# Two MLP down-projections computed with seven half-size matrix products instead of eight in most of their steps

## The chip, the cores and the metric

The kernel runs on one core of a Trainium2 chip. The metric is the device time of one execution in microseconds (us), of which several are timed and the median is given. TensorE multiplies matrices and accumulates in eight PSUM banks of 128 x 512 float32 values; VectorE (DVE in the profile) and ScalarE (ACT) do elementwise work; SyncE's queue (SP) starts the transfers from device memory. Each engine takes its instructions strictly from its own queue, and engines wait for each other through semaphores.

## The reference, cut to what matters

Two layers of a hybrid block act on x of 256 tokens by 1024 channels. Each layer mixes tokens (an mLSTM and two attentions) and then runs an MLP:

```python
mix = jnp.concatenate([hm, ha, hl], axis=-1)
x = x + mix @ w_out                                     # 1024 -> 1024
h2 = rms_norm(x, g_mlp_norm)
x = x + jnp.square(jax.nn.relu(h2 @ w_up)) @ w_down     # 1024 -> 4096 -> 1024
```

All of it is float32. The change is in the last product, `@ w_down`, alone.

## The kernel before, in words

**Three products for one.** TensorE is fed with a rounded float32 format. Each operand is therefore split in a high part (a rounded copy) and a low part (what the rounding left), and `mm3` (L192 to L195) issues three matmuls for one product: high x high (L193), low x high (L194) and high x low (L195). Every weight is split on the chip: `stream` has ScalarE write the high part `wh` (L182) and VectorE the low part `wl` (L183), 128 x 1024 values at a time, in the order in which the products take the pieces, up to six pieces ahead. The split pieces live in a ring of seven slots (`hlp`), which a piece leaves when its last matmul is through. The raw weights come from device memory in jobs of 1 MB (two pieces each) into three buffers `raw` (L165), on SyncE's queue.

**The MLP** is a loop of 18 rounds, j = 0 to 17. In rounds 0 to 15 a step of w_up makes 256 of the 4096 hidden channels: two blocks of 128 channels by 256 tokens, each a sum over 8 blocks of input channels, so 2 x 8 x 3 = 48 matmuls with 256 columns into one PSUM bank `up`. Then the hidden values are made: L931 (ACT) `rr` = relu(up), L932 (DVE) `hf` = max(up, 0) x rr, L933 (ACT) `hrh` = the rounded square, L934 (DVE) `hrl` = hf - hrh. In rounds 2 to 17 a step of w_down uses the hidden values made two rounds before (LAG = 2): two blocks b of 128 hidden channels, two halves m of the tokens, two halves n of the 1024 output channels, 2 x 2 x 2 x 3 = 24 matmuls with 512 columns. They accumulate over all 16 steps in four banks `acc`, one for each (m, n). So TensorE does step 0, 1, 2 of w_up, then w_down 0, w_up 3, w_down 1, and so on to w_down 14 and 15.

After the last step `update` (L947) scales each bank by r2, which holds the norm's factor per token, and adds it to the running x (`xs`). In the first layer TensorE goes on with transposes of xs (`xtp`, L327) and with `latp`, the first product of the next layer; `xh` and `xl` are the split halves of the transposed x. In the second layer the halves go to device memory.

**PSUM.** Four of the eight banks belong to the group "big" (here `acc`), four to "sm" (here `up` and `xtp`).

**Order of the work.** The program is written in the order above; a scheduler then sets the order in each engine's queue and places the waits, by what each instruction reads and writes and by when pool slots come free. The rows of that order are shown where a step of the prediction rests on them.

Of the kernel before, what the change touches and what calls it, by code (L numbers as in the profile page):

```python
# [10 lines left out]
F32 = mybir.dt.float32  # L11
F32R = mybir.dt.float32r
# [107 lines left out]
def hybrid_kernel(ctx: ExitStack, tc: tile.TileContext, x: bass.AP, xt: bass.AP, pos: bass.AP,  # L120
# [10 lines left out]
    def sb(shape, name, dt=F32, bufs=1, tag=None):  # L131
        return tp.tile([128] + list(shape), dt, name=name, tag=tag or name, bufs=bufs)
# [36 lines left out]

    def stream(i):  # L170
        while state["split"] < min(i + SPLIT_AHEAD + 1, len(pieces)):
            _, _, j, c, n = pieces[state["split"]]
# [3 lines left out]
            r = raw[j][:, c:c + n]  # L176
            if j == 0:
                hl[state["split"]] = (r,)
            else:
                h = hlp.tile([128, PW], F32R, name="wh", tag="wh")  # L180
                lo = hlp.tile([128, PW], F32R, name="wl", tag="wl")
                A.activation(h[:, :n], r, AF.Copy)  # L182
                V.tensor_sub(lo[:, :n], r, h[:, :n].bitcast(F32))  # L183
# [8 lines left out]
    def mm3(o, lh, ll, rh, rl, start, stop):  # L192
        T.matmul(o, lh, rh, start=start, stop=False)  # L193
        T.matmul(o, ll, rh, start=False, stop=False)  # L194
        T.matmul(o, lh, rl, start=False, stop=stop)  # L195
# [264 lines left out]
    for l in range(L):  # L460
# [444 lines left out]
        xh, xl, half = made_["x"]  # L905


        r2 = sb([2], "r2")
        acc = []
        hs = {}  # L910
        hrh = sb([4, 2, S], "hrh", F32R, tag="xh2")
        hrl = sb([4, 2, S], "hrl", F32R, tag="xl2")
        rr = sb([1024], "rr", tag="dB").rearrange("p (c b t) -> p c b t", c=2, b=2)
        hf_ = sb([2, 2, S], "hf", tag="yc")
        for j in range(16 + LAG):
            if j < 16:
                up = sm([2, S], "up")
                if j == 0:
# [5 lines left out]
                    acc = [big("acc") for _ in range(2)]  # L924
# [5 lines left out]
                r, hf, hh, hlo = rr[:, j % 2], hf_[:, j % 2], hrh[:, j % 4], hrl[:, j % 4]  # L930
                A.activation(r, up, AF.Relu)  # L931
                V.scalar_tensor_tensor(hf, up, 0.0, r, op0=OP.max, op1=OP.mult)  # L932
                A.activation(hh, r, AF.Square)  # L933
                V.tensor_sub(hlo, hf, hh.bitcast(F32))  # L934
                hs[j] = (hh, hlo)
            if j >= LAG:
                i = j - LAG
                ws = [weights(l, "dn", 2 * i + b) for b in range(2)]

                def bank(n, m):  # L940
                    down(acc[m][n], *hs[i], (0, 1), ws, m, n, i == 0, i == 15)

                def update(n, m):
                    w = 256 if l == L - 1 and (n, m) == NM[-1] else 512
                    for c0 in range(0, 512, w):
                        c = slice(n * 512 + c0, n * 512 + c0 + w)
                        V.scalar_tensor_tensor(xs[:, m, c], acc[m][n][:, c0:c0 + w], r2[:, m:m + 1], xs[:, m, c],  # L947
                                               op0=OP.mult, op1=OP.add)
                        if l == L - 1:
                            nc.sync.dma_start(out[:, m, c], xs[:, m, c])  # L950

                if i < 15:
                    for n, m in NM:
                        bank(n, m)
                else:
                    made = last_rows(bank, update, None if l == L - 1 else pr[l + 1][:, P_MIX:P_MIX + 8])

# [70 lines left out]
```

## Time and profile before

| what | value |
|---|---|
| median of 3 runs | 624.45 us (624.13 to 624.69) |
| the profiled execution's own time | 624.25 us |
| its span, from first to last instruction | 622.5 us |
| granted TensorE clock | 1.00 |
| TensorE busy (PE) | 611.1 us, 98% |
| weight loads into TensorE (PEld) | 542.9 us, 87% |
| VectorE busy (DVE) | 398.6 us, 64% |
| ScalarE busy (ACT) | 334.8 us, 54% |
| weight splits on VectorE (L183) | 196 instructions, 233.4 us |

A row of a timeline gives the start in us from the start of the span, the duration, the engine, line, operation, tiles and shapes, how many instructions are merged in the row, and in brackets how long the engine had idled before and what ended that. Matmuls and elementwise instructions overlap their neighbours on the same engine: the next one starts before the recorded end of the one before. In this text the time from one start to the next, of instructions that wait for nothing, is called the **pitch**.

### The profile page before, as it was taken

How to read it: one execution, taken by the hardware profiler on the slowest of the kernel's cores; microseconds unless marked ns; L12 is line 12 of the kernel's file. 1: busy time of each engine (PE TensorE's matmuls, PEld its weight loads, DVE VectorE, ACT ScalarE, POOL GpSimd, SP SyncE). 2: the span in 40 equal slices, each digit the busy share in tenths (PEclk: the TensorE clock that was granted, in tenths of full speed). 3: DMA queues.
4: the chain of work that ended last, by engine and by line, in shares of the span. 5: the costliest groups of instructions: out<-in, count | busy, mean ns of one | idle time of the engine just before them, and what ended most of it. 6: DMA issues, size and time to landing. Idle time of an engine off the chain costs nothing.

```text
span 622.5 us, 9831 instructions
## 1 busy us (share of the span) xinstructions
PE 611.1 (98%) x3850; PEld 542.9 (87%) x3850; DVE 398.6 (64%) x759; ACT 334.8 (54%) x565; POOL 39.6 (6%) x91
## 2 busy tenths in 40 slices
PE   6999999999999999999999999999999999999997
PEld 5988878889998989989899897888998998988985
DVE  4889876767555555555587996786765555555542
ACT  4876885465444444444367777653744444444430
POOL 7852000000000000000000000000000000000000
PEclk9999999999999999999999999999999999999999
DMA  8775221455465564654445642235456465564601
GB/s 294 300 301 197 101 102 69 151 188 203 144 207 192 181 222 139 211 195 169 159 149 215 204 136 73 98 111 185 179 185 218 140 211 195 171 221 151 203 2 67
DMA packets 17327, 106.39 MB, mean 171 GB/s; under 512 B 2304, under 2 KB 2816, under 8 KB 5504
## 3 DMA queue, kind: packets, MB, share of 16 engines
q1 hardware_dynamic: 16992, 105.75, 48.7%
q8 instruction: 30, 0.49, 0.3%
q14 instruction: 17, 0.14, 0.1%
q10 hardware_dynamic: 288, 0.02, 0.0%
HBM read 104.71 MB, written 1.05 MB: 170 GB/s over the span
## 4 chain that ended last, share of the span: by engine, by line
PE 89%; POOL 5%; DVE 3%; issue 1%; ACT 1%; DVEq 0%; POOLq 0%
PE acc L194 12%; PE acc L195 12%; PE acc L193 12%; PE up L193 9%; PE up L194 9%; PE up L195 9%; DVE wl L183 2%; PE vp L194 1%; PE op L193 1%; PE vp L193 1%; PE vp L195 1%; PE op L195 1%; PE op L194 1%; PE lsc L419 1%; PE qkp L194 1%
## 5 line engine op out<-in xcount | busy, mean ns | idle before, releaser
L183 DVE TENSOR_TENSOR wl<-raw,wh 128x1024 fp32r<-128x1024 f32 (+2 forms) x196 | 233.4, 1207 | 142.7 <-ACT wh L182 138.5
L182 ACT ACTIVATE wh<-raw 128x1024 fp32r<-128x1024 f32 (+2 forms) x196 | 200.3, 1043 | 173.9 <-PE acc L194 93.3
L193 PE MATMUL up<-xh,wh 128*128 128x256 f32 x480 | 134.2, 280 | 0.1
L194 PE MATMUL up<-xh,wl 128*128 128x256 f32 x480 | 134.0, 279 | 0.0
L195 PE MATMUL up<-xl,wh 128*128 128x256 f32 x480 | 133.9, 279 | 0.0
L195 PE MATMUL acc<-wl,hrh 128*128 128x512 f32 x256 | 101.3, 396 | 0.0
L193 PE MATMUL acc<-wh,hrh 128*128 128x512 f32 x256 | 101.3, 396 | 0.0
L194 PE MATMUL acc<-wh,hrl 128*128 128x512 f32 x256 | 101.3, 396 | 0.0
L193 PEld LDWEIGHTS up<-xh,wh 128*128 128x128 f32 x480 | 90.3, 188 | 1.7 <-PE xtp L327 0.5
L194 PEld LDWEIGHTS up<-xh,wl 128*128 128x128 f32 x480 | 90.2, 188 | 1.2
L195 PEld LDWEIGHTS up<-xl,wh 128*128 128x128 f32 x480 | 90.3, 188 | 0.0
L195 PEld LDWEIGHTS acc<-wl,hrh 128*128 128x128 f32 x256 | 48.1, 188 | 11.5
L194 PEld LDWEIGHTS acc<-wh,hrl 128*128 128x128 f32 x256 | 48.1, 188 | 10.3
L193 PEld LDWEIGHTS acc<-wh,hrh 128*128 128x128 f32 x256 | 48.1, 188 | 10.4
L931 ACT ACTIVATE rr<-up 128x512 f32<-128x512 f32 x32 | 19.1, 596 | 52.1 <-PE up L195 52.1
L932 DVE SCALAR_TENSOR_TENSOR hf<-up,rr 128x512 f32<-128x512 f32 x32 | 22.1, 691 | 33.2 <-ACT rr L931 33.2
L193 PE MATMUL acc<-wh,mh 128*128 128x512 f32 x64 | 25.9, 404 | 0.0
L195 PE MATMUL acc<-wl,mh 128*128 128x512 f32 x64 | 25.3, 396 | 0.0
L194 PE MATMUL acc<-wh,ml 128*128 128x512 f32 x64 | 25.3, 395 | 0.0
L934 DVE TENSOR_TENSOR hrl<-hf,hrh 128x512 fp32r<-128x512 f32 x32 | 21.9, 685 | 0.1
L933 ACT ACTIVATE hrh<-rr 128x512 fp32r<-128x512 f32 x32 | 19.8, 619 | 0.0
L193 PE MATMUL qkp<-xh,wh 128*128 128x256 f32 x64 | 18.6, 291 | 0.2 <-ACT scr L693 0.2
(351 smaller groups left out, 957.1 us busy)
## 6 DMA issues: line engine op xcount, KB each, us to landing
raw<-in_wts_dram SPq DMA_DIRECT2D x91, 1024.0 KB, 4.8
raw<-in_wts_dram SPq DMA_DIRECT2D x2, 740.0 KB, 5.7
raw<-in_wts_dram SPq DMA_DIRECT2D x2, 576.0 KB, 5.3
xts<-in_xt_dram SPq DMA_DIRECT2D x4, 256.0 KB, 4.4
raw<-in_wts_dram SPq DMA_DIRECT2D x4, 256.0 KB, 4.7
xs<-in_x_dram SPq DMA_DIRECT2D x1, 1024.0 KB, 10.5
raw<-in_wts_dram SPq DMA_DIRECT2D x2, 512.0 KB, 3.5
raw<-in_wts_dram SPq DMA_DIRECT2D x2, 478.0 KB, 7.0
```

The lines of the kernel that those rows point to most:

```text
L182: A.activation(h[:, :n], r, AF.Copy)
L183: V.tensor_sub(lo[:, :n], r, h[:, :n].bitcast(F32))
L193: T.matmul(o, lh, rh, start=start, stop=False)
L194: T.matmul(o, ll, rh, start=False, stop=False)
L195: T.matmul(o, lh, rl, start=False, stop=stop)
L419: T.matmul(sc[j][:, i], qT(2 * i + j, m), kT(2 * i + j, m + 1), start=False, stop=True, skip_group_check=True)
L931: A.activation(r, up, AF.Relu)
L932: V.scalar_tensor_tensor(hf, up, 0.0, r, op0=OP.max, op1=OP.mult)
L933: A.activation(hh, r, AF.Square)
L934: V.tensor_sub(hlo, hf, hh.bitcast(F32))
```

## The change

Write A for the hidden values of a step in four blocks, A(m, b) for token half m and channel block b, and B(b, n) for the weights. Before, each output quarter is C(m, n) = A(m, 0) B(0, n) + A(m, 1) B(1, n): eight products. In steps 0 to 13 of each MLP seven products of sums take their place (the form of Strassen's method with few additions that Winograd gave). With

- U4 = A(1,0) - A(0,0), U5 = A(0,1) - A(0,0), U6 = U4 + A(0,1), U7 = A(1,1) - U6,
- t0 = -B(0,0) - B(0,1), t1 = -B(0,1) - B(1,1), t2 = B(1,1) - t0, t3 = t2 + B(1,0),

the products are P1 = A(1,0) B(0,0), P2 = A(1,1) B(1,0), P6 = U6 t2, P7 = U4 t1, P4 = A(0,1) t3, P5 = U5 t0, P3 = U7 B(1,1), taken in this order, and C(1,0) = P1 + P2, C(0,0) = P4 + P1 - P6 - P7, C(0,1) = P5 - P1 + P6 + P7, C(1,1) = P3 + P5 - P1 + P6.

Each product has a PSUM bank of its own, in which it accumulates over the fourteen steps: P1, P2 and P6 in the group "sm", so that one bank is left there for `up`, the other four in "big". After step 13 the parts that several outputs share are added to xs (`into`); steps 14 and 15 are done with eight products as before, added into the banks P4, P2, P5 and P3, each of which by then holds what is still to be added of one quarter.

The sums of the weights (`dn_part`) and of the hidden values are made by VectorE. They are split in high and low parts afterwards, so that a step of w_down has four pieces: a (512 columns, B(0,0)), b (1024: B(1,1), B(1,0)), d (1024: t2, t3), c (1024: t0, t1). The hidden values are squared into float32 (`us`), seven blocks of 128 columns are formed and split into `hrh` and `hrl`; the step that made `hf` from the PSUM bank is gone. Ring, raw buffers, lookahead in pieces, and the bytes moved are unchanged.

```diff
+SEVEN = 14
+DN_PARTS = {"a": 512, "b": 1024, "d": 1024, "c": 1024, "e": 1024}
+LAST = (((0, 0), 4, ((0, "e", 0), (2, "b", 1))), ((0, 1), 2, ((1, "e", 0), (3, "b", 1))),
+        ((1, 0), 5, ((0, "e", 1), (2, "b", 0))), ((1, 1), 3, ((1, "e", 1), (3, "b", 0))))
+PRODUCTS = ((1, 0, "a", 0), (2, 2, "b", 1), (6, 5, "d", 0), (7, 3, "c", 1), (4, 1, "d", 1), (5, 4, "c", 0),
+            (3, 6, "b", 0))
...
-    return w["w_down"][pc[1] * 128:(pc[1] + 1) * 128]
+    b = w["w_down"][pc[1] * 256:(pc[1] + 1) * 256].reshape(2, 128, 2, 512)
+    return np.concatenate([b[0, :, 0], b[0, :, 1], b[1, :, 1], b[1, :, 0]], axis=1)
...
+                if pc[0] == "dn":
+                    pieces += [(l, (*pc, part), len(jobs), 0, DN_PARTS[part])
+                               for part in ("abdc" if pc[1] < SEVEN else "eb")]
...
+    def dn_part(j, part):
+        r = raw[j]
+        if part in "ae":
+            return r[:, :DN_PARTS[part]]
+        if part == "b":
+            return r[:, 1024:]
+        if part == "d":
+            t = sums[j] = sb([2048], "tsum", tag="mix")
+            V.scalar_tensor_tensor(t[:, :1024], r[:, :1024], -1.0, r[:, 512:1536], op0=OP.mult, op1=OP.subtract)
+            V.tensor_sub(t[:, 1024:1536], r[:, 1024:1536], t[:, :512])
+            V.tensor_add(t[:, 1536:], t[:, 1024:1536], r[:, 1536:])
+            return t[:, 1024:]
+        return sums.pop(j)[:, :1024]
...
+        us = [sb([8, 128], "us", tag=t) for t in ("yc", "qkT")]
...
+        def product(n, i, ai, part, bi, first, last):
+            if n not in prod:
+                prod[n] = ps.tile([128, 512], F32, name=f"P{n}", tag="sm" if n in (1, 2, 6) else "big", bufs=4)
+            wh, wl = weights(l, "dn", i, part)
+            hh, hlo = hs[i]
+            c = slice(bi * 512, bi * 512 + 512)
+            mm3(prod[n], hh[:, ai], hlo[:, ai], wh[:, c], wl[:, c], first, last, skip_group_check=n == 5)
...
-                V.scalar_tensor_tensor(hf, up, 0.0, r, op0=OP.max, op1=OP.mult)
-                A.activation(hh, r, AF.Square)
-                V.tensor_sub(hlo, hf, hh.bitcast(F32))
+                A.activation(u[:, 0:4].rearrange("p (b h) t -> p b (h t)", b=2), r, AF.Square)
+                if j < SEVEN:
+                    V.tensor_sub(u[:, 4:6], u[:, 1:3], u[:, 0:1].to_broadcast([128, 2, 128]))
+                    V.tensor_add(u[:, 6], u[:, 4], u[:, 2])
+                    V.tensor_sub(u[:, 7], u[:, 3], u[:, 6])
+                    src = u[:, 1:]
+                else:
+                    src = u[:, :4]
+                    hh, hlo = hh[:, :4], hlo[:, :4]
+                A.activation(hh, src, AF.Copy)
+                V.tensor_sub(hlo, src, hh.bitcast(F32))
...
+            i = j - LAG
+            if 0 <= i < SEVEN:
+                for p in PRODUCTS:
+                    product(p[0], i, *p[1:], i == 0, i == SEVEN - 1 and p[0] in (1, 6, 7))
+            if i == SEVEN - 1:
+                x1, u2, u3 = sb([512], "x1", tag="pa"), scratch(512), scratch(512)
+                A.activation(x1, prod[1], AF.Copy)
+                V.tensor_sub(u2, x1, prod[6])
+                V.tensor_sub(u3, u2, prod[7])
+                into(1, 1, prod[5])
+                into(0, 0, u3)
+                into(1, 0, x1)
+                into(0, 1, u3, -1)
+                into(1, 1, u2, -1)
+            if SEVEN <= i < 15:
+                for q in (0, 1, 3, 2):
+                    for p in LAST[q][2]:
+                        product(LAST[q][1], i, *p, False, False)
```

Two places of the order are shown. **The first** is VectorE's queue in one round of the steady part of an MLP. Before (here the split of a step's w_up pieces and of its w_down pieces read alike; four of them make a round):

```order
L183 TENSOR_TENSOR wl<-raw,wh 128x1024 x3
L932 SCALAR_TENSOR_TENSOR hf<-up,rr 128x512
L183 TENSOR_TENSOR wl<-raw,wh 128x1024
L934 TENSOR_TENSOR hrl<-hf,hrh 128x512
L183 TENSOR_TENSOR wl<-raw,wh 128x1024 x3
```

And with the change (`wl<-raw 128x1024 x2` are the w_up pieces of the next round but one, `tsum` the sums of the weights, `us` the sums of the hidden values, `wl<-tsum x2` the pieces d and c):

```order
L208 TENSOR_TENSOR wl<-raw,wh 128x1024 x2
L221 SCALAR_TENSOR_TENSOR tsum<-raw 128x1024
L994 TENSOR_TENSOR us<-us 128x256
L208 TENSOR_TENSOR wl<-raw,wh 128x512
L995 TENSOR_TENSOR us<-us 128x128
L208 TENSOR_TENSOR wl<-raw,wh 128x1024
L996 TENSOR_TENSOR us<-us 128x128
L222 TENSOR_TENSOR tsum<-raw,tsum 128x512
L223 TENSOR_TENSOR tsum<-tsum,raw 128x512
L1002 TENSOR_TENSOR hrl<-us,hrh 128x896
L208 TENSOR_TENSOR wl<-tsum,wh 128x1024 x2
```

Six instructions in a round have become thirteen; `us` follows the square of the round's own `up`, and `hrl` follows the rounding of those sums on ScalarE, whose queue holds in a round: relu, the high part of a, the square, the high part of b, the rounding of `us`, then the high parts of d, of c, and of the two w_up pieces.

**The second** is ScalarE's queue where the first layer's MLP ends and the second layer begins (`wh` of 888 columns and of 1024 are pieces of the second layer). Before:

```order
L182 ACTIVATE wh<-raw 128x888
L182 ACTIVATE wh<-raw 128x1024
L319 ACTIVATE xh<-xtp,par_75 128x256 x3
L182 ACTIVATE wh<-raw 128x1024
L319 ACTIVATE xh<-xtp,par_75 128x256
L182 ACTIVATE wh<-raw 128x888
L371 ACTIVATE scr,ssx<-xs 128x1024
L319 ACTIVATE xh<-xtp,par_75 128x256 x4
```

And with the change:

```order
L207 ACTIVATE wh<-raw 128x888
L207 ACTIVATE wh<-raw 128x1024 x2
L207 ACTIVATE wh<-raw 128x888
L359 ACTIVATE xh<-xtp,par_75 128x256 x4
L411 ACTIVATE scr,ssx<-xs 128x1024 x2
L359 ACTIVATE xh<-xtp,par_75 128x256 x4
```

The last two splits of weights now stand ahead of the first `xh`, and both sums of squares (`scr`) ahead of the second four. On TensorE the first transposes, which stood ahead of the last bank of w_down, stand behind it.

More of the change, by code (lines that the diff above doesn't have):

```diff
@@ L94, in piece_cols @@
         return {"uq": 384, "ukv": 512}[pc[0]] * (pc[2] - pc[1])
-    return 1024
+    return 2048 if pc[0] == "dn" else 1024
 def pack_piece(pc, w):
@@ L150, in hybrid_kernel @@
             for pc in group:
-                pieces.append((l, pc, len(jobs), c, piece_cols(pc)))
+                if pc[0] == "dn":
+                    pieces += [(l, (*pc, part), len(jobs), 0, DN_PARTS[part])
+                               for part in ("abdc" if pc[1] < SEVEN else "eb")]
+                else:
+                    pieces.append((l, pc, len(jobs), c, piece_cols(pc)))
                 c += piece_cols(pc)
@@ L155, in hybrid_kernel @@
     index = {(pc[0], pc[1]): i for i, pc in enumerate(pieces)}
-    raw, hl = {}, {}
+    raw, hl, sums = {}, {}, {}
     state = {"dma": 0, "split": 0}
@@ L171, in stream @@
         while state["split"] < min(i + SPLIT_AHEAD + 1, len(pieces)):
-            _, _, j, c, n = pieces[state["split"]]
+            _, pc, j, c, n = pieces[state["split"]]
             while state["dma"] < min(j + DMA_AHEAD + 1, len(jobs)):
@@ L176, in stream @@
             r = raw[j][:, c:c + n]
+            if pc[0] == "dn":
+                r = dn_part(j, pc[2])
             if j == 0:
@@ L190, in weights, with mm3 @@
         return hl[i]
[L192 to L195, printed above, removed]
+    def mm3(o, lh, ll, rh, rl, start, stop, **kw):
+        T.matmul(o, lh, rh, start=start, stop=False, **kw)
+        T.matmul(o, ll, rh, start=False, stop=False, **kw)
+        T.matmul(o, lh, rl, start=False, stop=stop, **kw)
     xts = sb([KT, S], "xts", tag="mix")
@@ L905, in hybrid_kernel, with into @@
         xh, xl, half = made_["x"]
-        r2 = sb([2], "r2")
-        acc = []
+        r2, nr2 = sb([2], "r2"), sb([2], "nr2")
+        prod = {}
         hs = {}
-        hrh = sb([4, 2, S], "hrh", F32R, tag="xh2")
-        hrl = sb([4, 2, S], "hrl", F32R, tag="xl2")
         rr = sb([1024], "rr", tag="dB").rearrange("p (c b t) -> p c b t", c=2, b=2)
-        hf_ = sb([2, 2, S], "hf", tag="yc")
+        us = [sb([8, 128], "us", tag=t) for t in ("yc", "qkT")]
+        hh2 = [sb([2, 7, 128], n, F32R, tag=t) for n, t in (("hrh", "xh2"), ("hrl", "xl2"))]
+        hh1 = [sb([7, 128], n, F32R, tag=t) for n, t in (("hrh", "tg"), ("hrl", "pb"))]
+        def product(n, i, ai, part, bi, first, last):
[5 more added lines that the diff above has]
+            mm3(prod[n], hh[:, ai], hlo[:, ai], wh[:, c], wl[:, c], first, last, skip_group_check=n == 5)
+        def into(m, n, src, sign=1, store=False):
+            g = (r2 if sign > 0 else nr2)[:, m:m + 1]
+            w = 256 if store and (m, n) == (1, 1) else 512
+            for c0 in range(0, 512, w):
+                c = slice(n * 512 + c0, n * 512 + c0 + w)
+                V.scalar_tensor_tensor(xs[:, m, c], src[:, c0:c0 + w], g, xs[:, m, c], op0=OP.mult, op1=OP.add)
+                if store:
+                    nc.sync.dma_start(out[:, m, c], xs[:, m, c])
         for j in range(16 + LAG):
@@ L923, in hybrid_kernel @@
                     V.reciprocal(r2, r2)
-                    acc = [big("acc") for _ in range(2)]
+                    V.tensor_scalar(nr2, r2, -1.0, None, op0=OP.mult)
                 else:
@@ L929, in hybrid_kernel @@
                             block(up[:, b], w, k * 128, k)
-                r, hf, hh, hlo = rr[:, j % 2], hf_[:, j % 2], hrh[:, j % 4], hrl[:, j % 4]
+                r, u = rr[:, j % 2], us[j % 2]
+                hh, hlo = [t[:, j % 3] for t in hh2] if j % 3 < 2 else hh1
                 A.activation(r, up, AF.Relu)
-                V.scalar_tensor_tensor(hf, up, 0.0, r, op0=OP.max, op1=OP.mult)
-                A.activation(hh, r, AF.Square)
-                V.tensor_sub(hlo, hf, hh.bitcast(F32))
@@ L935, in hybrid_kernel @@
-                hs[j] = (hh, hlo)
[L936 to L956, printed above, removed]
+                A.activation(u[:, 0:4].rearrange("p (b h) t -> p b (h t)", b=2), r, AF.Square)
@@ new lines, in hybrid_kernel, with bank, update @@
+            if SEVEN <= i < 15:
+                for q in (0, 1, 3, 2):
+                    for p in LAST[q][2]:
+                        product(LAST[q][1], i, *p, False, False)
+        def bank(n, m):
+            _, q, ps_ = LAST[NM.index((n, m))]
+            for b in range(2):
+                product(q, 15, *ps_[b], False, b == 1)
+        def update(n, m):
+            into(m, n, prod[LAST[NM.index((n, m))][1]], 1, l == L - 1)
+        made = last_rows(bank, update, None if l == L - 1 else pr[l + 1][:, P_MIX:P_MIX + 8])
```

3 lines of the change are left out of this document (2 added, 1 removed).

## The prediction

> **What bounds the kernel now.** First the page's totals and its chain of waits.
>
> ```profile
> span 622.5 us, 9831 instructions
> PE 611.1 (98%) x3850; PEld 542.9 (87%) x3850; DVE 398.6 (64%) x759; ACT 334.8 (54%) x565; POOL 39.6 (6%) x91
> PE 89%; POOL 5%; DVE 3%; issue 1%; ACT 1%; DVEq 0%; POOLq 0%
> ```
>
> TensorE holds 89% of the chain. But VectorE's 64% is a mean over the kernel, and the change loads VectorE in the MLPs alone. So next come stretches of the first MLP: a w_down step, a w_up step, and the next whole round (window, length, then busy time of PE, PEld, DVE, ACT).
>
> ```profile
> 229.73:235.33 5.60, 5.60 (x26) 4.51 (x25) 2.52 (x3) 2.80 (x4) 0.00 (x0) 1.00 0.54 190
> 235.33:240.93 5.60, 5.60 (x49) 5.60 (x48) 3.58 (x3) 2.33 (x3) 0.00 (x0) 1.00 0.54 181
> 240.93:252.13 11.20, 11.20 (x74) 10.11 (x73) 6.10 (x6) 5.13 (x6) 0.00 (x0) 1.00 0.56 187
> ```
>
> The 24 matmuls of a w_down step take 5.60 us, the 48 of a w_up step 5.60 us. A round is 11.20 us of unbroken TensorE; VectorE works 6.10 of it and ScalarE 5.13. The pitch of a w_down matmul is 5.60 / 24 = 0.233 us. VectorE's instructions overlap too, so I read their pitches from starts in timelines:
>
> ```profile
> 140.77 1.23 DVE L183 TENSOR_TENSOR wl<-raw,wh 128x1024 fp32r<-128x1024 f32 x1 [1.76 <-ACT wh L182]
> 141.91 0.68 DVE L932 SCALAR_TENSOR_TENSOR hf<-up,rr 128x512 f32<-128x512 f32 x1
> 142.51 1.22 DVE L183 TENSOR_TENSOR wl<-raw,wh 128x1024 fp32r<-128x1024 f32 x1
> ...
> 57.07 0.41 DVE L657 TENSOR_TENSOR lkl<-kpr,lrr_y 128x256 f32<-128x256 f32 x1
> 57.41 0.68 DVE L655 TENSOR_TENSOR lkl<-lkl,lks 128x512 f32<-128x512 f32 x1
> ...
> 54.59 0.28 DVE L402 TENSOR_TENSOR pps<-rpq 128x128 f32<-128x128 f32 x1
> 54.79 0.17 DVE L312 SCALAR_TENSOR_TENSOR lrr_t<-lrr_t,lvv 128x16 f32<-128x16 f32 x1
> ...
> 55.75 0.17 DVE L313 SCALAR_TENSOR_TENSOR lrr_y<-lrr_t,lrr_y 128x16 f32<-128x16 f32 x1
> 55.84 0.17 DVE L313 SCALAR_TENSOR_TENSOR mrr_y<-mrr_t,mrr_y 128x16 f32<-128x16 f32 x1
> ...
> 108.05 0.17 DVE L311 TENSOR_TENSOR nrr_t<-nrr_y 128x8 f32<-128x8 f32 x1
> 108.25 0.17 DVE L312 SCALAR_TENSOR_TENSOR nrr_t<-nrr_t,ssn 128x8 f32<-128x8 f32 x1
> ```
>
> 1024 columns recur after 1.14 us, 512 after 0.60, 256 after 0.34, 128 after 0.20. The last four rows show what a need of the instruction just ahead costs: independent neighbours start 0.09 us apart, a result's user 0.20 us after its maker, so 0.11 us more.
>
> **The change part by part.** *TensorE.* Each of steps 0 to 13 loses one product, three matmuls: 14 x 2 layers x 3 = 84, at 0.233 us, **19.6 us**. They lie on the chain with nothing beside them. A round would be 11.20 - 0.70 = 10.50 us, if the other engines keep up.
>
> *VectorE, the doubtful part.* By the rows of its queue a round now holds six instructions of 1024 columns (the splits of b, c, d and of two w_up pieces, and the first sum), three of 512 (split of a, two sums), one of 896, one of 256, two of 128. The pitch at 896 columns, on the line through 512 and 1024, is 0.60 + 0.54 x 384 / 512 = 1.01 us. Together 6 x 1.14 + 3 x 0.60 + 1.01 + 0.34 + 2 x 0.20 = 10.39, and 0.11 for the second sum, which needs the first just ahead: **10.50 us**, TensorE's own round. A dead heat, so the waits decide, and I lay out one round. The rows for ScalarE and the handover:
>
> ```profile
> 240.82 0.28 PE L195 MATMUL up<-xl,wh 128*128 128x256 f32 x1
> 240.93 0.39 PE L193 MATMUL acc<-wh,hrh 128*128 128x512 f32 x1
> ...
> 241.13 0.60 ACT L931 ACTIVATE rr<-up 128x512 f32<-128x512 f32 x1 [1.74 <-PE up L195]
> 241.62 1.05 ACT L182 ACTIVATE wh<-raw 128x1024 fp32r<-128x1024 f32 x1
> 242.57 0.62 ACT L933 ACTIVATE hrh<-rr 128x512 fp32r<-128x512 f32 x1
> 245.79 2.01 ACT L182 ACTIVATE wh<-raw 128x1024 fp32r<-128x1024 f32 x2 [2.60 <-PE acc L194]
> ...
> 246.89 2.36 DVE L183 TENSOR_TENSOR wl<-raw,wh 128x1024 fp32r<-128x1024 f32 x2 [2.36 <-ACT wh L182]
> ```
>
> Let 0 be the first w_down matmul after a w_up step. Relu starts at 0.20, the high part of a at 0.69, the square at 1.19 (ends 1.81), the high part of b at 1.68 (pitches on ScalarE: 0.49 for 512, 0.95 for 1024; a waiting engine starts some 0.05 us after its releaser). VectorE: sum U4, U5 at 1.85, a 2.19, U6 2.79, b 2.99, U7 4.13, t2 4.33, t3 5.04 (ends 5.73), `hrl` 5.64 to 6.65. ScalarE can round t2 and t3 only then, 5.78 to 6.83, so the split of d starts at 6.88: **0.23 us of waiting**. Then c 8.02, w_up 9.16 and 10.30, t0 and t1 11.44, and the next U4 at 12.58, where TensorE's round would allow 1.85 + 10.50 = 12.35. VectorE falls 0.23 us behind per round: its own round is 10.73.
>
> That delays nothing while it has a lead. The tightest need is piece c: its low part, written 8.02 to 9.25, is read by the third matmul of the fourth product of the next step, at 10.50 + 9 x 0.233 + 0.47 = 13.07. **Lead 3.8 us** (d has 4.2, w_up pieces 5). The lag grows in 11 rounds, from the fourth `up` step to the fifteenth, by 2.5 us, and by the same count the first rounds leave about 0.35: 2.9 in all. So the lead holds with 0.9 us over, and VectorE's work is priced at nothing. If the cover is gone, each layer pays 11 x (round - 10.50) - 3.45 us.
>
> Bounds for VectorE's round: 10.50 without the wait; above, recorded durations laid end to end, with the 896 taken from 888:
>
> ```profile
> L183 DVE TENSOR_TENSOR wl<-raw,wh 128x1024 fp32r<-128x1024 f32 x186 | 224.5, 1224 | 138.5 <-ACT wh L182 134.3 <-PE mpt L435 3.0 <-PE mN L839 1.1
> L183 DVE TENSOR_TENSOR wl<-raw,wh 128x888 fp32r<-128x888 f32 x4 | 4.3, 1081 | 3.8 <-ACT wh L182 3.8
> L934 DVE TENSOR_TENSOR hrl<-hf,hrh 128x512 fp32r<-128x512 f32 x32 | 21.9, 685 | 0.1
> ```
>
> 6 x 1.224 + 3 x 0.685 + 1.09 + 0.41 + 2 x 0.28 + 0.23 = 11.69 us. I take 10.73, because the rows in which VectorE runs without a break are these very shapes.
>
> The Trainium skill, VectorE: DVE Perf Modes, section "The DRAIN you can't avoid", says that the next instruction does not start until the pipe of the one before has emptied, and refers to another section for instructions that start earlier. By that rule alone rounds would be 11.69 us and the time that of the third rival below. The trace disagrees: 1.14 us from start to start where the duration is 1.23.
>
> *ScalarE* goes from 5.13 to five of 1024 (0.95), three of 512 (0.49) and one of 896 (about 0.83): 7.1 us of 10.50, hidden. *PSUM:* `up` has one bank left, so a w_up step must wait for the relu of the one before; that is over at 0.20 + 0.60 = 0.80, the bank is wanted at 4.90. The 4.1 us between hide it; without them it would cost 0.8 us x 28 = 22 us. *Transfers:* the same megabytes; t0 to t3 hold a raw buffer until 5.73 instead of its split, and the next load into it is wanted some 12 us later against 4.8 to land:
>
> ```profile
> raw<-in_wts_dram SPq DMA_DIRECT2D x91, 1024.0 KB, 4.8
> ```
>
> *After step 13* seven VectorE instructions of 512 columns, some 5 us, lie beside the 11.2 us of steps 14 and 15.
>
> *Where the layers meet* TensorE loses a little. Before:
>
> ```profile
> 314.05 1.07 ACT L182 ACTIVATE wh<-raw 128x1024 fp32r<-128x1024 f32 x1
> 315.35 0.96 ACT L182 ACTIVATE wh<-raw 128x888 fp32r<-128x888 f32 x1
> ...
> 317.76 0.19 PEld L349 LDWEIGHTS latp<-xh,wh 128*128 128x128 f32 x1 [0.34 <-ACT xh L319]
> ```
>
> These two splits wait for w_down's last pieces and now stand ahead of the first `xh`, while the transposes follow the last bank. With them at 0.95 + 0.85 us behind the release, the first `xh` comes about 0.7 us after TensorE is ready; the 0.34 us idle of before is covered by products placed there. Net +0.4; bounds 0 and 2 (both splits plus a `latp` wait). The starts of the MLPs I take as even: VectorE's first sums stand in front of two additions to xs, but TensorE has w_up matmuls to do meanwhile.
>
> **Sum:** 19.6 - 0.4 = 19.2 us less. The profiled execution took 624.25, of which 1.75 lies around the span; it would take 605.0 with a span of 603.3. The median is 0.2 above it: **605.3 us**.
>
> **The rivals.**
>
> *VectorE runs out of lead.* With a round of 10.9 to 11.4 us (a few more waits of 0.1 to 0.2), at 11.15 each layer pays 11 x 0.65 - 3.45 = 3.7: **612.7 us**. For: a dead heat, thirteen instructions with waits. Against: before, the waits ahead of `wl` in the rows above cost nothing while VectorE was busy.
>
> *Every VectorE instruction waits for its predecessor to finish, slower than before.* Place: the sums and splits of one round. Price: 0.11 us at each of the twelve places where I count an overlap, a round of 10.73 + 1.32 = 12.05; each layer pays 17.05 - 3.45 = 13.6, so **632.5 us**. It is slower from a round of 11.68 us on (19.15 / 2 = 9.6 to lose per layer, + 3.45, over 11). For: most of the sums wait for VectorE's own earlier results. Against: the 0.11 us shows only between direct neighbours.
>
> *Durations end to end*, 11.69 us: each layer pays 9.6, **624.6 us**, no change.
>
> *The saving is not had*, because seven products that change bank every three matmuls pitch slower. At 0.26 us, 28 x 21 x 0.027 = 16 us come back: **621 us**. Against: the step from the last w_down matmul to `up`, another bank, shows no gap in the rows above. Lost cover of the `up` bank would end near 627, and is counted with the slower one.
>
> **How the numbers follow.** Forecast 0.66, lead runs out 0.20, slower 0.07, end to end 0.04, pitch 0.03. About 0.2% (1.2 us) can be told from no change. Faster: 0.66 + 0.20 + 0.03 = 0.89; within: 0.03; slower: 0.08, as end to end falls on both sides. The forecast's own range is 604.3 to 607; down to 604 nothing but the matmuls is gained, and up to 614 more than half of the second case is in.
>
> **What would show it.** Right: 3766 PE matmuls instead of 3850, w_down steps of 4.90 us, rounds of 10.50 with PE unbroken, VectorE busy for over 10.2 us of each and its U4 later every round. Wrong: TensorE idle behind `wl` at the fourth product, growing from mid-MLP; rounds over 10.7; TensorE behind `rr` at the start of a w_up step; over 2 us idle where the layers meet.

## The result, and the profile after

| | before | after |
|---|---|---|
| median of 4 runs | 624.5 us (624.13 to 624.69) | 606.65 us (606.64 to 606.84) |
| span of the profiled execution | 622.5 us | 604.9 us |
| first MLP, first w_down step to w_down step 13 (13 rounds) | 145.61 us | 137.31 us |

The ratio is 0.9716, with a 95% interval of 0.9699 to 0.9732. The forecast was 605.3, so 17.85 of the 19.2 us came. The page of the changed kernel, its totals and its chain of waits:

```profile
span 604.9 us, 9950 instructions
PE 592.9 (98%) x3766; PEld 532.5 (88%) x3766; DVE 529.3 (88%) x967; ACT 400.9 (66%) x655; POOL 39.7 (7%) x91
PE 75%; DVE 14%; POOL 5%; issue 4%; ACT 2%; DVEq 0%; ACTq 0%; POOLq 0%
```

The 84 matmuls are gone (3766 against 3850). But VectorE's share of the chain went from 3% to 14%, while TensorE is still busy in 98% of the span: in the MLPs two engines run almost level, as the last of the next rows shows (10.61 us of TensorE, 10.39 of VectorE). Stretches of the first MLP (columns as in the prediction: window, length, busy PE, PEld, DVE, ACT, POOL, granted clock), a w_up step, a w_down step and a whole round:

```profile
229.64:235.40 5.76, 5.76 (x50) 5.75 (x49) 5.54 (x8) 4.58 (x5) 0.00 (x0) 1.00 0.65 243
235.40:240.27 4.87, 4.87 (x24) 3.94 (x23) 4.87 (x7) 2.79 (x5) 0.00 (x0) 1.00 0.43 128
235.40:246.01 10.61, 10.61 (x72) 9.68 (x70) 10.39 (x14) 7.21 (x10) 0.00 (x0) 1.00 0.54 193
```

Two of three rounds start 10.54 us apart, the third 10.61. TensorE doesn't pause in them, and yet the parts aren't the forecast's: w_up, which the change doesn't touch, takes 5.75 us instead of 5.60, and a w_down step 4.79 (every third 4.87) instead of 4.90. VectorE in the same stretch:

```profile
226.66 1.22 DVE L221 SCALAR_TENSOR_TENSOR tsum<-raw 128x1024 f32<-128x1024 f32 x1
...
230.28 0.68 DVE L222 TENSOR_TENSOR tsum<-raw,tsum 128x512 f32<-128x512 f32 x1
230.99 0.69 DVE L223 TENSOR_TENSOR tsum<-tsum,raw 128x512 f32<-128x512 f32 x1
231.60 1.08 DVE L1002 TENSOR_TENSOR hrl<-us,hrh 128x896 fp32r<-128x896 f32 x1
232.87 2.36 DVE L208 TENSOR_TENSOR wl<-tsum,wh 128x1024 fp32r<-128x1024 f32 x2 [0.18 <-ACT wh L207]
235.15 2.35 DVE L208 TENSOR_TENSOR wl<-raw,wh 128x1024 fp32r<-128x1024 f32 x2
237.42 1.22 DVE L221 SCALAR_TENSOR_TENSOR tsum<-raw 128x1024 f32<-128x1024 f32 x1
```

From first sum to first sum 10.76 us, with one wait of 0.18 for ScalarE at the split of d: the predicted 10.73 and 0.23. Last, the end of the first MLP, from w_down step 13 to the next layer's first product, before and after (one row of each kernel's stretches), and what TensorE waits for there:

```profile
296.93:314.60 17.67, 17.67 (x83) 14.36 (x82) 9.93 (x12) 7.61 (x11) 0.00 (x0) 1.00 0.43 137
```

```profile
288.24:306.62 18.38, 17.58 (x79) 13.54 (x77) 18.38 (x22) 12.28 (x17) 0.00 (x0) 1.00 0.58 214
```

```profile
296.29 0.68 DVE L1011 TENSOR_TENSOR scr<-x,P 128x512 f32<-128x512 f32 x1
296.89 0.75 DVE L970 SCALAR_TENSOR_TENSOR xs<-P,r,xs 128x512 f32<-128x512 f32 x1
...
297.69 0.50 PE L233 MATMUL P<-wh,hrh 128*128 128x512 f32 x1 [0.30 <-DVE xs L970]
```

This stretch has three matmuls less than before and is 0.71 us longer. VectorE is busy in all 18.38 us of it. Its first instruction of the additions after step 13 starts at 296.29, 8 us after step 13 began, and a matmul of step 14 waits for the bank P5 that one of them empties.

The spans differ by 17.6 us. Against the forecast of 19.2: the 26 rounds between the first and the last of the fourteen steps give 16.6 instead of 18.2 (1.6 less); the end of the first MLP loses 0.7 where it should gain 0.3 (1.0 less); the start, the second layer's mixing stages and the end of the second MLP together gain 1.0 more (0.39, 0.38, 0.25).

### The profile page after: what moved, and what is told of

Its sections match the earlier page's. It is cut to its first block, busy times and chain, and to the rows that moved or that the text cites. A ratio compares the mean times of both kernels' runs of the same rounds, so it can differ in the third digit from the quotient of the medians.

```text
span 604.9 us, 9950 instructions
## 1 busy us (share of the span) xinstructions
PE 592.9 (98%) x3766; PEld 532.5 (88%) x3766; DVE 529.3 (88%) x967; ACT 400.9 (66%) x655; POOL 39.7 (7%) x91
## 4 chain that ended last, share of the span: by engine, by line
PE 75%; DVE 14%; POOL 5%; issue 4%; ACT 2%; DVEq 0%; ACTq 0%; POOLq 0%
DVE wl L208 8%; PE up L233 7%; PE up L234 7%; PE up L235 7%; PE P L233 6%; PE P L234 6%; PE P L235 6%; PE acc L235 2%; PE acc L233 2%; PE acc L234 2%; ACT wh L207 1%; PE vp L234 1%; PE op L233 1%; PE vp L233 1%; PE vp L235 1%
## 5 line engine op out<-in xcount | busy, mean ns | idle before, releaser
L233 PE MATMUL P<-wh,hrh 128*128 128x512 f32 x228 | 89.5, 393 | 0.3 <-DVE xs L970 0.3
L234 PE MATMUL P<-wh,hrl 128*128 128x512 f32 x228 | 89.3, 392 | 0.0
L235 PE MATMUL P<-wl,hrh 128*128 128x512 f32 x228 | 89.0, 390 | 0.0
L208 DVE TENSOR_TENSOR wl<-tsum,wh 128x1024 fp32r<-128x1024 f32 x56 | 66.3, 1222 | 6.1 <-ACT wh L207 6.1
L207 ACT ACTIVATE wh<-tsum 128x1024 fp32r<-128x1024 f32 x56 | 56.4, 1050 | 14.2 <-DVE tsum L223 14.2
L235 PEld LDWEIGHTS P<-wl,hrh 128*128 128x128 f32 x228 | 42.8, 188 | 9.5
L233 PEld LDWEIGHTS P<-wh,hrh 128*128 128x128 f32 x228 | 42.9, 188 | 9.1 <-DVE xs L970 0.7
L234 PEld LDWEIGHTS P<-wh,hrl 128*128 128x128 f32 x228 | 42.9, 188 | 8.1
L1002 DVE TENSOR_TENSOR hrl<-us,hrh 128x896 fp32r<-128x896 f32 (+1 forms) x32 | 33.2, 1036 | 4.1 <-ACT hrh L1001 4.1
L221 DVE SCALAR_TENSOR_TENSOR tsum<-raw 128x1024 f32<-128x1024 f32 x28 | 34.1, 1218 | 0.0
```

Of the source, the lines that this page charges most:

```text
L221: V.scalar_tensor_tensor(t[:, :1024], r[:, :1024], -1.0, r[:, 512:1536], op0=OP.mult, op1=OP.subtract)
L233: T.matmul(o, lh, rh, start=start, stop=False, **kw)
L234: T.matmul(o, ll, rh, start=False, stop=False, **kw)
L235: T.matmul(o, lh, rl, start=False, stop=stop, **kw)
L1002: V.tensor_sub(hlo, src, hh.bitcast(F32))
```

## The experiments

### Why a step slowed that wasn't touched

Two things could reach w_up: the heavier traffic of VectorE and ScalarE, or the place of its operands. The built programs tell the place. The change adds the two-element tile `nr2`, and with it `raw`, `wh` and `wl`, which are allocated last, start 32 bytes further: at a multiple of 256 bytes in a partition, where before they stood 224 past one. `xh`, `xl` and the first two pairs of `hrh` and `hrl` stand at multiples of 256 in both. Two theories, then: T (traffic) and P (place).

**Places by the step.** Edit:

```diff
-                h = hlp.tile([128, PW], F32R, name="wh", tag="wh")
-                lo = hlp.tile([128, PW], F32R, name="wl", tag="wl")
+                o = place(lay, pc)
+                h = hlp.tile([128, PW + 32], F32R, name="wh", tag="wh")[:, o:o + PW]
+                lo = hlp.tile([128, PW + 32], F32R, name="wl", tag="wl")[:, o:o + PW]
```

> The changed kernel, with every weight buffer 128 bytes longer, and the piece of each step placed at its own distance from a multiple of 64 bytes: w_up's pieces in steps 1 to 15 at 0, 4, 8, 16, 24, 32, 36, 48, 56, 60, 64, 80, 96, 112, 124 bytes, w_down's in steps 0 to 13 at 0, 32, 0, 16, 48, 32, 4, 60, 16, 8, 24, 48, 64, 96. In the second MLP xh and xl, and two of three pairs of hrh and hrl, stand 32 bytes further as well. Theory P (placement): TensorE's pitch goes by where its two operands start: w_up steps at 0 and 64 bytes take 5.75 us, at 32 and 96 bytes 5.60; w_down steps at 0 and 64 take 4.79 where hrh starts at 0, and 4.90 at 32 and 96; the values between tell the grain. Theory T (traffic): VectorE's and ScalarE's heavier reading slows w_up, and then all w_up steps are alike, 5.75 us, and all w_down steps 4.79 to 4.87 as in the changed kernel.

Measured, in a single run: 608.17 us. Stretches of this kernel: the w_up steps at 32, 36 and 64 bytes, then the w_down step at 4:

```profile
188.42:194.13 5.71, 5.71 (x49) 5.71 (x48) 5.49 (x7) 4.86 (x5) 0.00 (x0) 1.00 0.57 220
199.01:204.58 5.57, 5.57 (x49) 5.57 (x48) 5.35 (x8) 4.86 (x5) 0.00 (x0) 1.00 0.66 227
241.14:246.83 5.69, 5.69 (x49) 5.68 (x48) 5.47 (x7) 4.10 (x5) 0.00 (x0) 1.00 0.66 245
215.12:220.11 4.99, 4.99 (x23) 3.98 (x22) 4.99 (x7) 2.78 (x5) 0.00 (x0) 1.00 0.45 141
```

The steps differ, so theory T falls: the same work beside them gives 5.57 or 5.71. Theory P in its form falls too: no step shows 5.75 at 0 or 64, and 32 isn't the fast one. The buffers of this kernel, 4224 bytes each, no longer lie alike modulo 256, so each step mixes distances; what it shows is that place alone moves a step by up to 0.14 us. That 4 bytes can do it (32 to 36) isn't shown: the pieces of these two steps also lie in other buffers of the ring.

**The ring shifted by 32 bytes,** in the changed kernel and in the one before. Edit, in both:

```diff
+    padp = ctx.enter_context(tc.tile_pool(name="padp", bufs=1))
+    V.memset(padp.tile([128, 8], F32, name="pad", tag="pad"), 0.0)
     rawp = ctx.enter_context(tc.tile_pool(name="raw", bufs=DMA_AHEAD + 1))
```

> The changed kernel with 32 unused bytes ahead of the raw, wh and wl buffers, so that these start at 32 past a multiple of 64 bytes, as they do before the change, instead of at 0. Theory P (placement): w_up steps 5.60 us, w_down steps 4.90, rounds 10.50, as the prediction had them; in all 1900 matmuls with a weight as the stationary operand gain 3.3 ns each, 6.2 us, and the matmuls with a weight as the moving operand give about 5 back: 605.6 us. Theory T (traffic of VectorE and ScalarE): nothing moves, w_up 5.75, w_down 4.79, 606.7 us.

Measured: 608.18 us (ratio 0.9743, 0.9728 to 0.9757), w_up 5.68, w_down 4.90 (every third 4.87): neither theory's time.

> The kernel before with the same 32 bytes, which bring its raw, wh and wl buffers to a multiple of 64 bytes. Theory P: its w_up steps go from 5.60 to 5.75 us, its w_down steps from 5.60 to 24 x 0.228 = 5.47, rounds 11.22, and the time stays at 623.5 to 624.5. Theory T: 5.60 and 5.60, 624.5.

Measured: 623.64 us (0.999, 0.998 to 1.000). The kernel before, with its weights at 0; a w_up step, a w_down step, a round:

```profile
223.96:229.71 5.75, 5.75 (x49) 5.75 (x48) 3.59 (x3) 2.36 (x3) 0.00 (x0) 1.00 0.53 181
229.71:235.18 5.47, 5.47 (x27) 4.51 (x25) 2.52 (x3) 2.77 (x4) 0.00 (x0) 1.00 0.55 193
229.71:240.93 11.22, 11.22 (x74) 10.26 (x73) 6.11 (x6) 5.13 (x6) 0.00 (x0) 1.00 0.53 188
```

To the hundredth what placement foretold, without one sum on VectorE (6.11 us busy): the place makes w_up slow and w_down fast. In the shifted changed kernel w_down agreed and w_up, at 5.68, did not return to 5.60, since 32 isn't 224. So I put the theory anew: what counts is the distance of a matmul's two operands from each other, modulo 256.

**The distances of before, in the changed kernel** (the same edit with 56 values in place of 8):

> The changed kernel with 224 unused bytes ahead of raw, wh and wl: these then start at the same distance from a multiple of 256 bytes (224) as before the change, and the order of the instructions is that of the changed kernel. Theory R (only the distance of TensorE's two operands from each other, modulo 256 bytes, sets its pitch): the pitches of before return, w_up 5.60 us, w_down 4.90, rounds 10.50 as the prediction had them (where both starts at 0 gave 5.75 and 4.79, and 32 gave 5.68 and 4.90). Time 605.5 to 607. Rival (something else in the changed kernel, its traffic for one, slows w_up): 5.68 to 5.75, 608.

Measured: 607.38 us (0.9725, 0.9711 to 0.9740). A w_up step, and the end of the first MLP from step 13:

```profile
230.20:235.81 5.61, 5.61 (x49) 5.61 (x48) 5.39 (x7) 3.82 (x4) 0.00 (x0) 1.00 0.64 244
288.24:307.82 19.58, 17.71 (x80) 13.53 (x78) 19.58 (x23) 13.46 (x18) 0.00 (x0) 1.00 0.59 220
```

Step 14 by itself, and TensorE's wait in it for the bank P5:

```profile
293.13:300.37 7.24, 5.83 (x25) 4.43 (x24) 7.24 (x10) 4.98 (x7) 0.00 (x0) 1.00 0.95 353
```

```profile
298.87 0.50 PE L235 MATMUL P<-wh,hrh 128*128 128x512 f32 x1 [1.41 <-DVE xs L972]
```

Rounds of 10.50, w_up 5.60, w_down 4.90 (every third 4.86): the prediction's own world, and it is *no faster* than the changed kernel as it stands (the intervals of the two ratios overlap). In each MLP its 13 rounds are 0.94 us shorter (136.37), but the end of the first MLP is 1.2 us longer, VectorE busy in all 19.58 us. In the first MLP, then, a faster TensorE was paid back at the end, to VectorE. The second MLP, behind which no layer follows, pays back only 0.2 us; what it gains is lost elsewhere, mostly ahead of the first w_down step (it starts at 151.87 us instead of 150.93), where the products have their old distances too.

### VectorE's lead

**One sum done twice.** Edit: the line `V.tensor_add(t[:, 1536:], ...)` of `dn_part` stands twice.

> The changed kernel with the last of the three sums of w_down's blocks (512 columns) done twice in each of the 14 steps: VectorE's round goes from 10.76 us to about 11.4, against TensorE's 10.55. Theory L (a lead that is used up): piece c is ready 3.7 us ahead of need in step 3 and falls behind by 0.8 us in each round, so TensorE begins to wait behind wl at the fourth product about step 7 or 8, and each layer pays 4 (counted from the measured lead) to 5.9 us (11 x (11.4 - 10.55) - 3.45): 614 to 618.5. Rival 1 (VectorE is the bound already, with no lead left): all of 28 x 0.6 = 17 us shows, 623. Rival 2 (VectorE is nowhere near it): under 607.5.

Measured: 637.37 us (1.0215, 1.0198 to 1.0233), outside every range. VectorE's first sums, a round apart, and that round:

```profile
238.42 1.23 DVE L221 SCALAR_TENSOR_TENSOR tsum<-raw 128x1024 f32<-128x1024 f32 x1
239.68 0.69 DVE L222 TENSOR_TENSOR tsum<-raw,tsum 128x512 f32<-128x512 f32 x1
240.40 0.69 DVE L223 TENSOR_TENSOR tsum<-tsum,raw 128x512 f32<-128x512 f32 x1
241.13 0.69 DVE L224 TENSOR_TENSOR tsum<-tsum,raw 128x512 f32<-128x512 f32 x1
...
250.23 1.22 DVE L221 SCALAR_TENSOR_TENSOR tsum<-raw 128x1024 f32<-128x1024 f32 x1
```

```profile
240.42:252.22 11.80, 11.17 (x71) 9.45 (x70) 11.53 (x15) 7.41 (x9) 0.00 (x0) 1.00 0.51 179
```

The added instruction moved the scheduler's whole order: the sums now follow each other directly and pay 0.1 us each for it, matmuls that need `wl` were put further back in TensorE's order, and VectorE's round is 11.81 us, not 11.4. With that round the prediction's formula gives 11 x (11.81 - 10.55) - 3.45 = 10.4 us per MLP; the thirteen rounds of each MLP grew by 11.4 (148.74 against 137.31). So the formula comes within 1 us for the rounds, though with TensorE's order changed this is no clean test of it. What it leaves out is again the end: from step 13 to the next layer 24.0 us against 18.4.

### Both bounds moved

**Best known distances.** The changed kernel with `xh` and `xl` 32 bytes further in the MLPs (w_up's operands at 224 from each other, w_down's at 0), the third pair of `hrh` and `hrl` at 0 as well, and the bank P5 emptied first. Edit, its core:

```diff
-        h = sb([KT, S], "xh", F32R)
-        lo = sb([KT, S], "xl", F32R)
+        h, lo = (sb([KT * S + 64], n, F32R)[:, s:s + KT * S].rearrange("p (k t) -> p k t", k=KT) for n in ("xh", "xl"))
...
+                into(1, 1, prod[5])
                 V.tensor_sub(u2, x1, prod[6])
                 V.tensor_sub(u3, u2, prod[7])
-                into(1, 1, prod[5])
```

> The changed kernel with three edits: in the MLPs xh and xl stand 32 bytes further, so that wh and wl lie at 224 past them modulo 256, as before the change, while w_down's operands stay at 0 against each other; the third pair of hrh and hrl is brought to a multiple of 256 bytes as well; the addition to xs that frees bank P5 goes first after step 13. The order on TensorE and ScalarE is the changed kernel's. Theory R: w_up 5.60 us, all w_down steps 4.77, rounds 10.37; 2 x 2.4 us from w_up, 0.8 from the third pair, 0.3 to 0.8 from P5, 600.3 in all. It also tests the lead: TensorE's round of 10.37 against VectorE's 10.76 lets VectorE fall 0.39 us behind per round instead of 0.20, which uses 3.5 us in nine rounds of a lead of 3.7 in step 3: if the lead is what I measured, TensorE still doesn't wait behind wl before the last steps. Rival (VectorE is the bound): rounds stay at 10.55 or above, 605.

Measured: 606.09 us (0.9704, 0.9689 to 0.9718), not told apart from the changed kernel. A w_up step, a round, the w_down steps 11 and 12, the end of the MLP, and TensorE's wait in step 14:

```profile
228.66:234.26 5.60, 5.60 (x50) 5.60 (x48) 5.38 (x8) 3.08 (x4) 0.00 (x0) 1.00 0.55 209
234.26:244.65 10.39, 10.39 (x72) 9.55 (x71) 10.17 (x14) 6.96 (x9) 0.00 (x0) 1.00 0.57 195
265.42:270.32 4.90, 4.90 (x24) 3.87 (x23) 4.81 (x5) 4.90 (x8) 0.00 (x0) 1.00 0.51 201
275.92:281.12 5.20, 5.10 (x24) 3.87 (x23) 5.01 (x6) 5.20 (x8) 0.00 (x0) 1.00 0.57 206
286.72:306.99 20.27, 17.64 (x79) 13.45 (x77) 20.09 (x23) 14.16 (x19) 0.00 (x0) 1.00 0.62 219
```

```profile
297.46 0.50 PE L233 MATMUL P<-wh,hrh 128*128 128x512 f32 x1 [1.50 <-DVE xs L970]
```

The pitches came as foretold (5.60, every w_down step 4.78, rounds 10.38), and the time didn't. The lead lasted to step 10 and ran out in steps 11 and 12 (4.90 and 5.20 where 4.78 is free); the end of the first MLP grew from 18.38 to 20.27 us. The rounds gained 1.75 us in each MLP (135.56 against 137.31). VectorE took 1.9 us back at the end of the first. At the end of the second 0.9 us are lost as well, but not to VectorE: TensorE's part of it takes 16.06 us against 16.00, and the rest comes behind the last addition to `xs`. What emptying P5 first is worth by itself was not tested.

**The same distances in the kernel before** (weights at 0, `xh` and `xl` at 32):

> The kernel before with the same placement: raw, wh and wl at 0, and xh and xl 32 bytes further in the MLPs. Theory R: w_up 5.60 us, w_down 5.47 (24 x 0.228), rounds 11.07; 2 x 2.4 us less than with all at 0 (623.6): 618.8. The gain of the seven products at equal placement is then 618.8 - 600.3 = 18.5, of which 0.8 + 0.5 are the two other edits. Rival: 623.6 (only the absolute start of a weight counts).

Measured: 619.15 us (0.9915, 0.9898 to 0.9931), w_up 5.60, w_down 5.47, rounds 11.07. Five microseconds from two shifts by 32 bytes (4.5 of them, 623.64 to 619.15, from that of `xh` and `xl`), where TensorE alone is the bound.

**VectorE relieved, three ways.** First the sums U4 to U7 on GpSimd (`G.` for `V.` in three lines), with the best distances and in the changed kernel as it is:

> The kernel of the last run (operands placed for the shorter pitches) with the sums U4 to U7 moved from VectorE to GpSimd, which has nothing to do in the MLPs; TensorE's order is the same. Theory E (VectorE's backlog is what each MLP pays at its end): VectorE's round falls from 10.76 us by 0.34 + 0.20 + 0.20 and the 0.1 to 0.2 of dependent starts to 9.9 to 10.0, below TensorE's 10.37, so there is no backlog: no wait behind wl in steps 11 and 12 (0.5 us per MLP), none for the addition that frees P5 (1.5 us), and the first transposes of the next layer aren't late; 602 to 603. Rival 1 (VectorE isn't what the end of the MLP waits for): 605.5 to 606. Rival 2 (GpSimd takes the sums so slowly, 96 columns take 0.43 to 1.06 us there, or slows VectorE so much beside it, that hrh is late or VectorE's round grows): 608 or more.

> The changed kernel as it is, with U4 to U7 on GpSimd. TensorE's round stays at 10.55 us (placement untouched). Theory E: only the ends gain, 0.4 us from the wait for P5 and what the transposes at the layer's end wait: 605.5 to 606. Rival 1: 606.65, unchanged. Rival 2 as above: slower, 608 or more.

Measured: 608.71 (0.9743, 0.9729 to 0.9758) and 609.13 us (0.9749, 0.9733 to 0.9766): rival 2. GpSimd and then VectorE, in the first of them:

```profile
239.68 0.92 POOL L994 TENSOR_TENSOR us<-us 128x256 f32<-128x256 f32 x1 [6.38 <-ACT us L992]
240.67 1.32 POOL L995 TENSOR_TENSOR us<-us 128x128 f32<-128x128 f32 x1
242.07 1.33 POOL L996 TENSOR_TENSOR us<-us 128x128 f32<-128x128 f32 x1
250.27 4.01 POOL L994 TENSOR_TENSOR us<-us 128x256 f32<-128x256 f32 x1 [6.87 <-ACT us L992]
```

```profile
239.91 1.76 DVE L221 SCALAR_TENSOR_TENSOR tsum<-raw 128x1024 f32<-128x1024 f32 x1
241.60 1.48 DVE L208 TENSOR_TENSOR wl<-raw,wh 128x1024 fp32r<-128x1024 f32 x1
243.00 0.95 DVE L222 TENSOR_TENSOR tsum<-raw,tsum 128x512 f32<-128x512 f32 x1
...
250.74 1.22 DVE L221 SCALAR_TENSOR_TENSOR tsum<-raw 128x1024 f32<-128x1024 f32 x1
```

While GpSimd sums, VectorE's 1.22 us become 1.76 and 1.48, its 0.69 become 0.95. In the last row of each view it is the other way round: the GpSimd sum takes 4.01 us where one of the same shape took 0.92, and VectorE's sum beside it keeps its 1.22. VectorE's rounds stay at 10.71 to 10.83 us, although three sums have left its queue. The Trainium skill, SBUF — State Buffer, section "Who interferes with whom", says that a VectorE instruction with two SBUF inputs contends with a GpSimd instruction that reads SBUF; these rows agree. The same section of the Trainium skill says that nothing but this port pair is contended for; TensorE's pitches above depend on where its operands lie, which that doesn't cover.

Second, the best distances without the sums of the weights:

> The kernel with the operands placed for the shorter pitches (606.1 us) without the three sums of w_down's blocks: pieces d and c are split from raw weights, so the seven products are of the wrong sums; everything else, TensorE's order included, stays. VectorE loses 1.14 + 0.60 + 0.72 us a round, 10.76 to about 8.2, with no other engine loaded in its place. Theory E (VectorE's backlog is paid at the end of each MLP): rounds of 10.37 to the last, no wait behind wl in steps 11 and 12 (0.5 us per MLP), none for P5 (1.5 us), the transposes not late: 602 to 603. Rival 1 (the end of the MLP waits for something else): 605.5 to 606.

Measured: 600.54 us (0.9614, 0.9599 to 0.9630), a larger gain than theory E asked for: rounds of 10.39 us to the last, and 17.59 us for the end of the first MLP. Third, complete, with only VectorE's order changed (ScalarE's follows: it rounds t2 and t3 ahead of `us`). Edit, in `dn_part`:

```diff
+        def total():
             t = sums[j] = sb([2048], "tsum", tag="mix")
...
+        if part == "b" and seven:
+            total()
         if part == "b":
             return r[:, 1024:]
         if part == "d":
-            return t[:, 1024:]
+            return sums[j][:, 1024:]
```

> The same kernel (606.1 us), complete, with the three sums of w_down's blocks written ahead of the split of piece b instead of ahead of d's. In VectorE's order the second and third sum then no longer follow their makers directly, and between the third sum and d's split stand two short sums and b's split, so that ScalarE has rounded t2 and t3 by then. Theory E: VectorE's round loses the wait of 0.19 and 0.1 to 0.2 of dependent starts, 10.76 to 10.4, which is TensorE's own 10.37: no backlog, 602 to 603.5. Rival 1: 605.5 to 606. Rival 3 (VectorE's round is the pitches alone and the wait counts for nothing, since it only moves elsewhere): rounds of VectorE still 10.7, 605.5 to 606.

Measured: 600.90 us (0.9617, 0.9603 to 0.9630). VectorE's first sums of two rounds, in the earlier one with the second sum right behind; then the same of a later round, with the split of d between; then that round and the end of the first MLP:

```profile
193.44 1.22 DVE L219 SCALAR_TENSOR_TENSOR tsum<-raw 128x1024 f32<-128x1024 f32 x1
194.69 0.69 DVE L220 TENSOR_TENSOR tsum<-raw,tsum 128x512 f32<-128x512 f32 x1
...
203.92 1.22 DVE L219 SCALAR_TENSOR_TENSOR tsum<-raw 128x1024 f32<-128x1024 f32 x1
...
234.24 1.21 DVE L219 SCALAR_TENSOR_TENSOR tsum<-raw 128x1024 f32<-128x1024 f32 x1
...
240.19 2.35 DVE L208 TENSOR_TENSOR wl<-tsum,wh 128x1024 fp32r<-128x1024 f32 x2
...
244.60 1.22 DVE L219 SCALAR_TENSOR_TENSOR tsum<-raw 128x1024 f32<-128x1024 f32 x1
```

```profile
234.06:244.45 10.39, 10.39 (x71) 9.55 (x70) 10.39 (x14) 7.34 (x9) 0.00 (x0) 1.00 0.57 203
286.00:303.59 17.59, 17.14 (x79) 13.60 (x77) 16.18 (x20) 11.17 (x15) 0.00 (x0) 1.00 0.56 193
```

VectorE's round has no wait left. It takes 10.48 us in most rounds, where the second sum still stands right behind the first, and 10.36 where a split stands between them; TensorE's takes 10.39. The two are level, no step waits behind `wl`, none waits for P5, and the end of the first MLP takes 17.59 us instead of 20.27, although VectorE does all its work. Against the run with the distances alone the span is 5.1 us shorter: 2.7 of them at this end, 1.0 in the rounds, 1.2 at the end of the second MLP and 0.2 at the start. This version beats both kernels: 5.75 us below the changed one. Last, the order alone, with the operands where the change put them:

> The changed kernel with the order edit of the last run alone (the three sums written ahead of the split of piece b), its operands where the change put them. Two bounds that lie side by side: TensorE's round stays at 10.55 us by its placement (w_up 5.75, w_down 4.79, every third 4.87), VectorE's falls from 10.76 to about 10.4, so only the ends of the MLPs gain: 0.3 to 0.4 us for P5 and some 0.2 to 0.4 at the transposes of the first MLP; 605.6 to 606.2, as the placement alone gave 606.1, where both together gave 600.9. Rival (the order alone is worth most of the 5.7 us): 602 or less.

Measured: 606.07 us (0.9704, 0.9690 to 0.9718). The end of the first MLP:

```profile
288.17:305.77 17.60, 17.15 (x80) 13.62 (x78) 15.58 (x19) 11.18 (x15) 0.00 (x0) 1.00 0.56 193
```

Distances alone (with P5 emptied first) 606.09, order alone 606.07, both 600.90: neither edit is worth more than 0.6 us while the other engine holds the round.

## Why the prediction was right or wrong

**The removed matmuls: right.** 3766 are left, and TensorE never pauses in the rounds that lost them.

**Their pitch and the pitch of the rest: mis-sized.** The term "84 x 0.233" took 0.233 for every w_down matmul and 5.60 for w_up as fixed. A tile of two values moved the weights by 32 bytes; w_up became 0.15 us slower per step and w_down 0.08 faster on the mean, rounds 10.56 instead of 10.50. Over 26 rounds that is the 1.6 us lost in the rounds. No row that the prediction used could have shown it; the addresses in the built program could have shown that something moves.

**VectorE's round: right,** 10.76 against 10.73, and with it the wait (0.18 against 0.23). The sum of its pitches, 10.39 without the dependent start and 10.50 with it, was met by the reordered kernel's 10.36 and 10.48. The Trainium skill, VectorE: DVE Perf Modes, section "The DRAIN you can't avoid", says that the next instruction does not start until the pipe is empty, and refers to another section for those that start earlier. The trace disagrees with the first of these: durations end to end would make a round of 11.69 us, and it took 10.76.

**The lead: right for the products.** No step of the changed kernel waits behind `wl`. Piece c's low part ends at 278.27 for step 12, which starts at 277.70 and whose fourth product reads it 2.5 us later, at 280.22: 1.9 us of lead left, where 0.9 was counted.

**"VectorE's work is priced at nothing": wrong, and this is the step that failed.** The prediction asked only when a product would wait for VectorE, not what VectorE owes when the steps end. It set the additions after step 13 beside the 11.2 us of steps 14 and 15; but VectorE comes there with its backlog and with the splits that stand ahead of them, and P5, in which step 14 must go on, is wanted after eighteen of its 24 matmuls. The price in the changed kernel is 18.38 - 17.60 = 0.8 us at the end of the first MLP (the order alone removes it). Where the forecast's pitches hold, that end takes 19.58 us where 17.37 was forecast (17.67 - 0.70 + 0.40): 2.2 us, as much as that kernel's 607.4 lies above 605.3 (the other stretches differ by up to 0.6 us either way and cancel). Of the 2.2 us, 1.6 are VectorE's: step 14 takes 7.24 us, where 24 matmuls at 0.233 take 5.60. The other 0.6 belong to the next point. So the nearness of 606.65 to the forecast is partly luck: a slower TensorE round hid some of VectorE's backlog, and faster products elsewhere gave 1.0 us that wasn't counted. That this is placement too is supported by the runs: `acc` of the mixing stage went from 396 to 390 ns, is back at 395 in the changed kernel with the distances of before, and goes to 391 in the kernel before with its weights at 0.

**Where the layers meet: right in kind, too small.** Without VectorE's backlog TensorE still idles 17.59 - 17.14 = 0.45 us there. But the stretch is also longer than forecast: at the reordered kernel's pitch the forecast's 17.37 us become some 17.0 (69 matmuls, 0.005 less each), and it took 17.59. So by this estimate the meeting costs 1.0 us where 0.4 was forecast, inside the bounds of 0 and 2.

**ScalarE, the single bank of `up`, transfers: right.** ScalarE works 7.21 us of a round (7.1 forecast), and TensorE nowhere waits for `rr` or for a transfer in the MLPs.

**The rivals.** "VectorE runs out of lead" was the right mechanism at the wrong place: it ran out at the end of the MLP, and, once TensorE was made faster, in steps 11 and 12. The rivals with rounds of 11.69 and 12.05 us fall by the measured 10.76. That bank changes cost nothing stands: at the forecast's distances the step took the 4.90 us of 21 matmuls at 0.233.

## What to carry to other kernels

When a change fills a second engine up to the first one's round, a lag that no product feels is still owed: follow it to the end of the loop, to whatever that engine must do before the next stage may start. With two engines level, an edit to one of them shows almost nothing, so a null result doesn't clear it; move both before judging either. And compare the start addresses of a matmul's operands when an untouched stage changes speed: a small new tile can shift everything allocated behind it.

## What the runs showed of the hardware that was not expected

TensorE's pitch depends on how far the two operands of a matmul lie from each other within a partition, modulo 256 bytes, at a granted clock of 1.00. Steps of 48 matmuls with 256 columns: 5.60 us with the stationary operand at 224 from the moving one, 5.75 at 0, 5.68 at 32; moving either operand to reach 224 does the same. The built programs put the distance at 224 modulo 512 in the kernel before and at 480 in the changed kernel with 224 bytes ahead, and both take 5.60, which is why 256 is called the period. Products with 512 columns: 0.228 us at 0 (4.79 / 21 and 5.47 / 24), 0.233 with the moving operand at 224 or 32 from the stationary one. Three distances were held for whole kernels; the mixed steps of the first experiment range from 5.57 to 5.71 us, and no rule for them was found. In the held kernels all matmuls of a step have one distance, so they can't tell a matmul's own two operands from one's moving operand and the next one's stationary operand. What in the chip does it stays open. For the kernel before, the better distances alone are worth 5.2 us (624.37 in the same runs against 619.15).
